# Down projection of a decoder step: second weight parts one slot later, one accumulator in two PSUM tiles by turns, weight loads two pairs ahead, last convolution later

## The chip, the cores and the metric

The program runs on one core of a Trainium2 chip. The metric is the device time of one execution in microseconds (us). Five engines work side by side, each through its own queue in program order: TensorE (PE; its weight loads are shown as PEld), VectorE (DVE), ScalarE (ACT), GpSimd (POOL) and SyncE (SP). SP issues nearly all DMAs of the stage that matters here. Engines wait for one another through semaphores.

## The reference, cut to what matters

One layer of a decoder step for 512 prompt rows and 8 x 8 sample rows, 576 rows in all, held transposed: 128 features on the partitions, 576 rows (two halves of 288) along the free axis. The attention half of the layer is untouched. The stage in question is the end of the channel mixer:

```python
    u = _rms(x, p['g_ffn']) @ p['w_up']
    up = jnp.concatenate([prev.astype(u.dtype), u], axis=1)
    c = p['conv_b'] + p['conv_w'][CONV_W - 1] * up[:, CONV_W - 1:]
    for j in range(CONV_W - 1):
        c = c + p['conv_w'][j] * up[:, j:j + T]
    a, b = jnp.split(c, 2, axis=-1)
    return x + (jax.nn.silu(a) * b) @ p['w_down'], up[:, T:]
```

`w_down` is 5632 x 2048 in float32, and the products have to keep float32's accuracy.

## The kernel before, in words

**Numbers in two parts.** TensorE multiplies in float32r. Each weight tile and each operand is therefore split in a first part (`whi`, a copy on ACT, lines 2217 to 2222, `down_first`) and a second part (`wlo`, source minus first part on DVE, lines 2224 to 2229, `down_second`). A product of a 512 x 128 weight block with a 512 x 288 operand block is three passes of four matmuls: first part with first part, first part with the operand's second part, second part with first part (`down_product`, line 2231). The second part of the weights is read by the third pass alone.

**Up projection, and the joint.** The loop over f = 0..43 in `finish` computes the up projection, convolution and gate. The convolution of f - 1 runs during f; that of f = 43 (`convolve(43, i)`, five steps on ACT, DVE and POOL) follows the loop. Then comes `down`.

**First 512 rows of w_down.** In `down` (line 2496) a loop over `ot` = 0..15 multiplies the first 512 rows directly, 24 matmuls for each `ot`, and adds the result to `hT`. It also prepares the operands of the first chunk (`build(1)`, its steps in the list `todo`).

**The other 5120 rows.** They are five chunks of 1024 rows. Each chunk has eight pairs of output tiles (256 output columns), 40 pairs in all, n = 0..39. A pair is a 2 x 2 x 2 block product done in seven products instead of eight, P1 P6 P5 P7 P2 P3 P4 in this order, 280 slots t in all, with i = t % 7 the place in the pair. Weight blocks: A11, A12 (one 512 KB load into a `raw` buffer of two), A21, A22 (256 KB loads into the shared `z` ring of eight), and four sums on DVE: S1 = A21 + A22, S2 = S1 - A11, S3 = A22 - S2, S4 = A12 - S2 (`down_sum`; S1, S3 and S4 overwrite a block that is no longer needed). P1 takes A11, P6 S2, P5 S1, P7 S3, P2 A12, P3 S4, P4 A22.

**Accumulators.** PSUM holds three of them, `Z[0]` to `Z[2]`: P1 and P2 add in bank 0, P6, P7 and P4 in bank 1, P5 and P3 in bank 2. After every product DVE adds the accumulator as it stands to the rows of `hT` where it belongs (`down_evict`; the result of P1 goes to a tile `Y`, in the first chunk by ACT, later by DVE). The next product of the same bank waits for that. Z[0] and Z[1] are the two tiles `zp`, Z[2] is one of four tiles `fa`.

**One slot t of the loop.** The program order is: first part of the weights of t + 2 (ACT), eviction of product t - 1 (DVE), second part of t + 2 (DVE), a weight sum (DVE, at i = 0, 2, 4, 5), one step of `todo` in seven of eight pairs (i = 3, 6; the operands of the next chunk, on DVE and ACT), at i = 1 the loads for pair n + 1 (SP), then the twelve matmuls of t. In the last chunk each pair also puts out its two tiles (`store_y`: transposes on TensorE into free `fa` tiles, copies, DMA).

The order of each queue is thus written out by the loop; a small clock in the program (`pump`) places only the output's steps.

Of the kernel before, what the change touches and what calls it, by code (L numbers as in the profile page):

```python
# [9 lines left out]
F32 = mybir.dt.float32  # L10
# [10 lines left out]
HB = 288  # L21
# [257 lines left out]
class Kern:  # L279
# [2138 lines left out]
    def finish(self, es, outs, w_down):  # L2418
        nc, a = self.nc, self.a
        self.fpool = self.pool(es, "ffn", side="right")  # L2420
        self.bpool = self.pool(es, "big", side="right")
        self.spawn(self.ffn_consts())
        self.cst, self.ssq, self.W = [None, None], None, {}
        self.B = {name: [[self.operand(name, n, half) for half in range(2)] for n in "hl"]
                  for _, name, _ in self.PRODUCTS.values()}
        order = [o for i in range(8) for o in (i, i + 8)]

        def xload(n):
            if n < 16:
                x = self.z("xr")  # L2430
                nc.sync.dma_start(out=x, in_=self.xT[order[n]])
                return x

        def free(kt):
            if kt == 0:
                self.weights(0, "A11")
                self.weights(0, "A22")
            elif kt in (1, 2):
                self.weights(0, ("A12", "A21")[kt - 1])
            elif kt == 6:  # L2440
                self.U = [self.place(12 + s, (128, FW), "u") for s in range(2)]
                for U in self.U:
                    nc.gpsimd.memset(U[:, 0:2], 0.0)
            elif kt == 7:
                self.C = [self.place(14 + s, (128, FW - 2), "C") for s in range(2)]
                self.first_parts(0, 0)
                self.second_parts()

        def later(kt):
            if kt == 4 and self.rest:  # L2450
                self.rest()
                self.rest = None

        x, self.rest = xload(0), None
        for n, ot in enumerate(order):
            last = n == 15
            ps, = self.gemm([(outs[ot], 128, list(range(8)), self.mixs)],
                            on_kt=lambda kt: (later(kt), last and free(kt)), before=self.mixed)
            nx = xload(n + 1)
            self.out_done(ot, ps, x)  # L2460
            x = nx
        self.rest()
        norm = self.spawn(self.second_norm(), first=True)
        self.Z = [self.zp(), self.zp(), self.ps("fa")]
        self.held.add(self.Z[2].tensor.name)
        self.gs, self.hT = [], {}
        self.gd = self.dram("gd", (128, 44, NT))
        self.st = Stream(self, 2, 4)
        downs = self.add_down(w_down, 0)
        self.w_down = w_down  # L2470
        win = a["win_sample"].rearrange("l b t k g d -> (l b) t (k g d)")
        todo = []
        for f in range(44):
            for i in range(7):
                if f == 0 and i == 3:
                    self.until(lambda: norm.done and not self.threads)
                parts = self.before_slot(f, i)
                if i > 3 and todo:
                    todo.pop(0)()
                self.product(f, i, parts)  # L2480
                if f == 43 and i in (0, 1):
                    todo += self.load_first(i)
            if 2 <= f < 18:
                b, t = (f - 2) // 2, 252 * (f % 2)
                nc.gpsimd.dma_start(out=win[b, t:t + 252],
                                    in_=a["cache_win"][0, b, 8 + t:260 + t].rearrange("t k g d -> t (k g d)"))
        while todo:
            todo.pop(0)()
        self.evict(43, 6)
        for i in range(5):  # L2490
            self.convolve(43, i)
        self.done(self.Z[2])
        self.down(downs)
        self.drain()

    def down(self, downs):
        for ot in range(2):
            self.load_h(ot)
        self.V, self.vs = {}, {}
        Y4 = self.fpool.tile([128, 4, HB], F32, name="Y4", tag="prev")  # L2500
        Y1 = self.fpool.tile([128, HB], F32, name="Y1", tag="cw")
        self.Y = [Y4[:, i] for i in range(4)] + [self.rstd[:, :HB], self.rstd[:, HB:], Y1]
        todo, B = self.build(1)
        for ot in range(16):
            hi, lo = self.st.get(downs[ot])
            o = self.zp()
            for kt in range(4):
                for n, (w, x) in enumerate(((hi, 0), (lo, 0), (hi, 1))):
                    for h in range(2):
                        self.mm(o[:, 512 * h:512 * h + HB], w[:, kt], self.gs[h][x][:, kt],  # L2510
                                kt == 0 and n == 0, kt == 3 and n == 2)
                    if n < 2:
                        self.pump()
            self.st.prep_to(downs[ot] + 5)
            h = self.h2(self.hT[ot])
            self.nc.vector.tensor_tensor(h, self.halves(o), h, ALU.add)
            if ot + 2 < 16:
                self.load_h(ot + 2)
            if 0 < ot < 15:
                todo.pop(0)()  # L2520
            if ot == 11:
                self.down_weights(0, 1)
            elif ot == 13:
                self.down_weights(0, 0)
            elif ot == 14:
                self.down_sum(0, "S1")
                self.down_first(0)
                self.down_sum(0, "S2")
                self.down_second(0)
                self.down_first(1)  # L2530
        self.down_second(1)
        self.Z = [self.zp(), self.zp(), self.ps("fa")]
        self.held.add(self.Z[2].tensor.name)
        for t in range(280):
            n, i = t // 7, t % 7
            if t % 56 == 0 and t:
                B = nextB
            if t % 56 == 0 and t < 224:
                todo, nextB = self.build(2 + t // 56)
            self.down_first(t + 2)  # L2540
            if t:
                self.down_evict(t - 1)
            self.down_second(t + 2)
            for m, name in {0: ((n, "S3"),), 2: ((n, "S4"),), 4: ((n + 1, "S1"),), 5: ((n + 1, "S2"),)}.get(i, ()):
                self.down_sum(m, name)
            if n % 8 and i in (3, 6) and todo:
                todo.pop(0)()
            if i == 1:
                self.down_weights(n + 1, 1)
                self.down_weights(n + 1, 0)  # L2550
            self.down_product(t, B)
        self.down_evict(279)

# [75 lines left out]
```

## Time and profile before

| | us |
|---|---|
| median of 3 runs | 2978.86 (2977.79 to 2979.95) |
| the profiled execution | 2977.68 |
| its span, first to last instruction | 2975.9 |

| engine | busy us | share of the span |
|---|---|---|
| PE | 2880.6 | 97% |
| PEld | 2839.7 | 95% |
| DVE | 2221.1 | 75% |
| ACT | 1459.3 | 49% |
| POOL | 390.3 | 13% |

The mean granted TensorE clock is 0.993. In the page's forty slices PE is at nine tenths or more nearly everywhere, and at eight tenths in most of the last seven, with DVE at eight or nine there. Those slices are the seven-product loop, which begins at 2435.15 us of the span. The shares of the whole span say little about it, so the rows below are taken from that stretch and from the joint before it. In a timeline row the first number is the start, the second the length, both in us, then engine, operation, output and inputs, count, and in brackets the idle time before it with what ended it. Rows of matmuls overlap, because matmuls are pipelined; the distance between starts is what counts.

### The profile page before, as it was taken

How to read it: one execution, taken by the hardware profiler on the slowest of the kernel's cores; microseconds unless marked ns; L12 is line 12 of the kernel's file. 1: busy time of each engine (PE TensorE's matmuls, PEld its weight loads, DVE VectorE, ACT ScalarE, POOL GpSimd, SP SyncE). 2: the span in 40 equal slices, each digit the busy share in tenths (PEclk: the TensorE clock that was granted, in tenths of full speed). 3: DMA queues.
4: the chain of work that ended last, by engine and by line, in shares of the span. 5: the costliest groups of instructions: out<-in, count | busy, mean ns of one | idle time of the engine just before them, and what ended most of it. 6: DMA issues, size and time to landing. Idle time of an engine off the chain costs nothing.

```text
span 2975.9 us, 56967 instructions
## 1 busy us (share of the span) xinstructions
PE 2880.6 (97%) x21370; PEld 2839.7 (95%) x21370; DVE 2221.1 (75%) x4403; ACT 1459.3 (49%) x2863; POOL 390.3 (13%) x681
## 2 busy tenths in 40 slices
PE   8999999999999999999999999999999998888889
PEld 7999999999999999999999999999999998888889
DVE  4332456766476566468999999999999978888888
ACT  6443568666354555334544454454454534333333
POOL 3011131312301111200111111111110100000000
PEclk9999999999999999999999999999999999999999
DMA  8443333222554566755444543433433452342333
GB/s 246 130 113 82 107 102 89 88 83 78 139 157 126 177 207 220 244 174 176 125 133 124 144 134 110 126 99 109 122 101 109 137 188 81 105 117 79 101 92 109
DMA packets 560143, 385.79 MB, mean 130 GB/s; under 512 B 65477, under 2 KB 527893, under 8 KB 559613
## 3 DMA queue, kind: packets, MB, share of 16 engines
q1 hardware_dynamic: 537068, 308.29, 36.5%
q0 software_dynamic: 22768, 73.86, 7.5%
q8 instruction: 169, 2.77, 0.4%
q14 instruction: 106, 0.86, 0.1%
q10 hardware_dynamic: 32, 0.01, 0.0%
HBM read 316.51 MB, written 75.32 MB: 132 GB/s over the span
## 4 chain that ended last, share of the span: by engine, by line
PE 54%; DVE 10%; issue 5%; ACT 3%; POOL 1%; DMA 0%; ACTq 0%; DVEq 0%; POOLq 0%
PE zp L189 39%; PE fa L189 15%; DVE wlo L189 3%; ACT whi L189 2%; DVE hT L189 1%; DVE s L189 1%; DVE t L189 1%; DVE a L189 1%; DVE raw L189 1%; POOL ret_sample L189 0%; DMA raw<-w_down 0%; DVE B22l L189 0%; POOL mix L189 0%; DVE T2l L189 0%; DVE B11l L189 0%
## 5 line engine op out<-in xcount | busy, mean ns | idle before, releaser
L189 ACT ACTIVATE whi<-raw 128x512 fp32r<-128x512 f32 x588 | 356.0, 625 | 460.7 <-PE zp L189 242.4
L189 DVE TENSOR_TENSOR wlo<-raw,whi 128x512 fp32r<-128x512 f32 x584 | 398.2, 697 | 118.7 <-ACT whi L189 116.1
L189 PE MATMUL zp<-ah,whi 128*128 128x288 f32 (+1 forms) x2208 | 480.9, 299 | 2.1 <-ACT whi L189 1.9
L189 PE MATMUL zp<-al,whi 128*128 128x288 f32 (+1 forms) x2208 | 478.1, 298 | 0.1
L189 PE MATMUL zp<-ah,wlo 128*128 128x288 f32 x2176 | 473.8, 299 | 3.1 <-DVE wlo L189 3.1
L189 ACT ACTIVATE whi<-s 128x512 fp32r<-128x512 f32 x256 | 156.3, 631 | 437.0 <-DVE s L189 343.9
L189 PEld LDWEIGHTS zp<-ah,whi 128*128 128x128 f32 (+1 forms) x2208 | 356.3, 189 | 5.5 <-ACT whi L189 2.3
L189 PEld LDWEIGHTS zp<-ah,wlo 128*128 128x128 f32 x2176 | 351.4, 189 | 6.4 <-DVE wlo L189 3.9
L189 PEld LDWEIGHTS zp<-al,whi 128*128 128x128 f32 (+1 forms) x2208 | 354.7, 188 | 1.8 <-DVE al L189 0.3
L189 ACT ACTIVATE whi<-a 128x512 fp32r<-128x512 f32 x344 | 202.2, 625 | 122.5 <-DVE u L189 78.2
L189 DVE TENSOR_TENSOR wlo<-a,whi 128x512 fp32r<-128x512 f32 x344 | 225.2, 687 | 29.0 <-ACT whi L189 26.2
L189 DVE TENSOR_TENSOR wlo<-s,whi 128x512 fp32r<-128x512 f32 x256 | 168.6, 687 | 28.2 <-ACT whi L189 28.2
L189 PE MATMUL zp<-T2h,whi 128*128 128x288 f32 x576 | 105.3, 301 | 51.5 <-DVE hT L189 51.4
L189 DVE SCALAR_TENSOR_TENSOR C<-u,cw,C 128x592 f32<-128x592 f32 x176 | 146.4, 832 | 3.1
L189 PEld LDWEIGHTS zp<-T2h,whi 128*128 128x128 f32 x576 | 84.4, 189 | 57.6 <-issue 30.5
L189 DVE CUSTOM_DVE_ANT_0 P<-fa,th 128x256 f32<-128x256 f32 (+3 forms) x128 | 60.9, 488 | 63.6 <-PE fa L189 61.7
L189 PE MATMUL zp<-T2h,wlo 128*128 128x288 f32 x576 | 103.4, 301 | 0.0
L189 PE MATMUL zp<-B11h,wlo 128*128 128x288 f32 x576 | 100.6, 294 | 2.3 <-DVE wlo L189 2.3
L189 PE MATMUL zp<-B11h,whi 128*128 128x288 f32 x576 | 100.3, 294 | 1.3 <-ACT whi L189 1.3
L189 DVE TENSOR_TENSOR hT<-zp,hT 128x288 f32<-128x288 f32 (+1 forms) x191 | 90.4, 478 | 14.5 <-PE zp L189 11.8
L189 PE MATMUL zp<-T2l,whi 128*128 128x288 f32 x576 | 101.2, 296 | 0.0
L189 PE MATMUL zp<-B11l,whi 128*128 128x288 f32 x576 | 100.2, 294 | 0.0
(435 smaller groups left out, 6640.1 us busy)
## 6 DMA issues: line engine op xcount, KB each, us to landing
a<-w_up SPq DMA_DIRECT2D x264, 256.0 KB
raw<-w_in SPq DMA_DIRECT2D x102, 512.0 KB
raw<-w_down SPq DMA_DIRECT2D x48, 512.0 KB
raw<-w_up SPq DMA_DIRECT2D x44, 512.0 KB
a<-w_down SPq DMA_DIRECT2D x80, 256.0 KB
raw<-w_out SPq DMA_DIRECT2D x32, 512.0 KB
gd<-g POOLq DMA_DIRECT2D x44, 288.0 KB, 2.9
xr<-xT SPq DMA_DIRECT2D x32, 288.0 KB
```

The costliest lines, as they stand in the source:

```text
L189: return fn(*a, **kw)
```

## The change

Five edits, all in `finish` and `down`:

- The second part of a weight tile is made in slot t for t + 1 (`down_second(t + 1)`) and no longer for t + 2. First parts stay at t + 2.
- Bank 1 has two tiles by turns: `Z = [A, bs[n % 2], C]`, set after the eviction of the last product of the pair before. A and `bs[0]` are the `zp` tiles, `bs[1]` and C are `fa` tiles, so two `fa` tiles are left for the output's transposes instead of three.
- The loads of weights are issued for pair n + 2, `raw` at i = 5 and A21, A22 at i = 6, instead of all for n + 1 at i = 1. Pairs 0 and 1 are loaded at `ot` = 11 to 14.
- The convolution of f = 43 runs inside the first two rounds of the `ot` loop, after the preparation of the weights, instead of ahead of the loop. The tiles `Y` are placed after the loop for that reason.
- The sums S1, S2 of pair 0 and its first weight parts come after the `ot` loop instead of at `ot` = 14, and `build` for the next chunk stands after the slot's other work.

```diff
         self.evict(43, 6)
-        for i in range(5):
-            self.convolve(43, i)
         self.done(self.Z[2])
...
             self.st.prep_to(downs[ot] + 5)
+            for i in ((0, 1), (2, 3, 4))[ot] if ot < 2 else ():
+                self.convolve(43, i)
             h = self.h2(self.hT[ot])
...
-            if ot == 11:
-                self.down_weights(0, 1)
-            elif ot == 13:
-                self.down_weights(0, 0)
-            elif ot == 14:
-                self.down_sum(0, "S1")
-                self.down_first(0)
-                self.down_sum(0, "S2")
-                self.down_second(0)
-                self.down_first(1)
-        self.down_second(1)
-        self.Z = [self.zp(), self.zp(), self.ps("fa")]
-        self.held.add(self.Z[2].tensor.name)
+            if ot in (11, 12):
+                self.down_weights(ot - 11, 1)
+            elif ot in (13, 14):
+                self.down_weights(ot - 13, 0)
...
+        self.down_sum(0, "S1")
+        self.down_sum(0, "S2")
+        for t in range(2):
+            self.down_first(t)
+        self.down_second(0)
+        A, C = self.zp(), self.ps("fa")
+        self.held.add(C.tensor.name)
+        bs = self.zp(), self.ps("fa")
+        self.held.add(bs[1].tensor.name)
         for t in range(280):
             n, i = t // 7, t % 7
             if t % 56 == 0 and t:
                 B = nextB
-            if t % 56 == 0 and t < 224:
-                todo, nextB = self.build(2 + t // 56)
             self.down_first(t + 2)
             if t:
                 self.down_evict(t - 1)
-            self.down_second(t + 2)
+            if i == 0:
+                self.Z = [A, bs[n % 2], C]
+            self.down_second(t + 1)
             for m, name in {0: ((n, "S3"),), 2: ((n, "S4"),), 4: ((n + 1, "S1"),), 5: ((n + 1, "S2"),)}.get(i, ()):
                 self.down_sum(m, name)
+            if t % 56 == 0 and t < 224:
+                todo, nextB = self.build(2 + t // 56)
             if n % 8 and i in (3, 6) and todo:
                 todo.pop(0)()
-            if i == 1:
-                self.down_weights(n + 1, 1)
-                self.down_weights(n + 1, 0)
+            if i == 5:
+                self.down_weights(n + 2, 0)
+            elif i == 6:
+                self.down_weights(n + 2, 1)
             self.down_product(t, B)
```

DVE's queue from slot 5 of a pair into slot 2 of the next one, before (`s` is S2, then S4; `a` numbers are A21 and A22, A21 holding S1; `raw` is A11 or A12, later S3; `hT` rows are evictions; `t` and `T3l` are a step of `todo`):

```order
L189 TENSOR_TENSOR s_31266<-a_31187,raw 128x512
L189 TENSOR_TENSOR hT<-fa,hT 128x288
L189 TENSOR_TENSOR wlo<-s_31266,whi 128x512
L189 TENSOR_TENSOR t<-T1l,B11l 128x576
L189 TENSOR_TENSOR T3l<-t,T3h 128x576
L189 TENSOR_TENSOR hT<-zp,hT 128x288
L189 TENSOR_TENSOR wlo<-a_31187,whi 128x512
L189 TENSOR_TENSOR raw<-a_31189,s_31266 128x512
L189 TENSOR_TENSOR wlo<-raw,whi 128x512
L189 TENSOR_TENSOR hT<-zp,hT 128x288
```

The same place in the changed kernel:

```order
L189 TENSOR_TENSOR s_31265<-a_31153,raw 128x512
L189 TENSOR_TENSOR hT<-fa,hT 128x288
L189 TENSOR_TENSOR wlo<-raw,whi 128x512
L189 TENSOR_TENSOR t<-T1l,B11l 128x576
L189 TENSOR_TENSOR T3l<-t,T3h 128x576
L189 TENSOR_TENSOR hT<-fa,hT 128x288
L189 TENSOR_TENSOR wlo<-s_31265,whi 128x512
L189 TENSOR_TENSOR raw<-a_31155,s_31265 128x512
L189 TENSOR_TENSOR wlo<-a_31153,whi 128x512
L189 TENSOR_TENSOR hT<-zp,hT 128x288
L189 TENSOR_TENSOR wlo<-raw,whi 128x512
```

The second part of S2 stood one eviction behind the sum that makes S2; now the second part of A11, the step of `todo` and a further eviction stand between. The second part of S3 stood right behind its sum; now two rows stand between.

TensorE's queue in the first pair that uses the second tile of bank 1 (T2, T1 and T3 are the operands of P6, P5 and P7), as a difference:

```order
 L189 MATMUL zp<-B11h,wlo 128x288 x4
-L189 MATMUL zp<-T2h,whi 128x288 x4
-L189 MATMUL zp<-T2l,whi 128x288 x4
-L189 MATMUL zp<-T2h,wlo 128x288 x4
+L189 MATMUL fa<-T2h,whi 128x288 x4
+L189 MATMUL fa<-T2l,whi 128x288 x4
+L189 MATMUL fa<-T2h,wlo 128x288 x4
 L189 MATMUL fa<-T1h,whi 128x288 x4
```

P6, P7 and P4 of every second pair write another tile; no matmul is added or moved.

ACT's queue at the joint between the up projection and the `ot` loop (`C` rows are the convolution of f = 43, `whi` the first parts for the `ot` loop), as a difference:

```order
 L189 ACTIVATE T2h<-T2l 128x1152
-L189 ACTIVATE whi<-raw 128x512 x2
+L189 ACTIVATE whi<-raw 128x512 x5
 L189 ACTIVATE C<-u,cw 128x592 x2
-L189 ACTIVATE C<-C 128x592
-L189 ACTIVATE whi<-raw 128x512 x4
+L189 ACTIVATE whi<-raw 128x512
+L189 ACTIVATE C<-C 128x592
```

Three first parts have moved ahead of the two `C` rows, the third of which reads the third `raw` tile of the `ot` loop.

## Rows read from the trace of the kernel before

**Rows 1.** Busy time by stretch: the five chunks (us, then each engine, clock, DMA).
```profile
2435.15:2544.70 109.55, 93.78 (x674) 90.94 (x673) 88.45 (x158) 42.67 (x74) 0.00 (x0) 0.98 0.39 111
2544.70:2653.11 108.41, 94.30 (x674) 92.21 (x673) 92.04 (x166) 40.48 (x67) 0.00 (x0) 0.97 0.35 100
2653.11:2760.61 107.50, 94.39 (x675) 92.34 (x674) 91.91 (x166) 40.48 (x67) 0.00 (x0) 0.97 0.35 101
2760.61:2869.46 108.85, 94.57 (x674) 92.32 (x673) 92.31 (x166) 40.60 (x67) 0.00 (x0) 0.97 0.35 101
2869.46:2975.90 106.44, 99.81 (x754) 98.90 (x752) 89.72 (x184) 39.55 (x71) 0.00 (x0) 0.97 0.35 101
```

**Rows 2.** Waits of PE, 2435.15 to 2975.9 (total us, times, longest).
```profile
PE zp L189 <- DVE hT L189: 57.9, 39, 2.6
```

**Rows 3.** Timeline of PE, one pair (n = 4).
```profile
2489.99 0.69 PE L189 MATMUL zp<-B11h,whi 128*128 128x288 f32 x4
...
2491.05 0.69 PE L189 MATMUL zp<-B11h,wlo 128*128 128x288 f32 x4
2492.55 0.77 PE L189 MATMUL zp<-T2h,whi 128*128 128x288 f32 x4 [0.81 <-DVE hT L189]
...
2496.59 0.77 PE L189 MATMUL zp<-T3h,whi 128*128 128x288 f32 x4 [0.63 <-DVE hT L189]
...
2503.01 0.69 PE L189 MATMUL zp<-B11h,whi 128*128 128x288 f32 x4
```

**Rows 4.** Timeline of PE, a pair without a wait (n = 9), its start and end.
```profile
2558.06 0.69 PE L189 MATMUL zp<-B11h,whi 128*128 128x288 f32 x4
...
2569.17 0.69 PE L189 MATMUL zp<-B11h,whi 128*128 128x288 f32 x4
```

**Rows 5.** Timeline of DVE around the pair of rows 3.
```profile
2487.04 0.68 DVE L189 TENSOR_TENSOR wlo<-a,whi 128x512 fp32r<-128x512 f32 x1
2487.64 0.68 DVE L189 TENSOR_TENSOR a<-a,a 128x512 f32<-128x512 f32 x1
2488.24 0.45 DVE L189 TENSOR_TENSOR hT<-zp,hT 128x288 f32<-128x288 f32 x1
2488.61 0.68 DVE L189 TENSOR_TENSOR wlo<-raw,whi 128x512 fp32r<-128x512 f32 x1
...
2491.95 0.45 DVE L189 TENSOR_TENSOR hT<-zp,hT 128x288 f32<-128x288 f32 x1
...
2493.92 0.68 DVE L189 TENSOR_TENSOR raw<-a,s 128x512 f32<-128x512 f32 x1
2495.38 0.69 DVE L189 TENSOR_TENSOR wlo<-raw,whi 128x512 fp32r<-128x512 f32 x1 [0.78 <-ACT whi L189]
```

**Rows 6.** Waits of DVE, 2435.15 to 2870.
```profile
DVE wlo L189 <- ACT whi L189: 62.8, 124, 1.6
```

**Rows 7.** DVE's groups in chunks 2 to 4 (busy us, mean ns): steps of `todo`.
```profile
L189 DVE TENSOR_TENSOR t<-B22l,t 128x576 f32<-128x576 f32 x6 | 4.5, 752 | 0.0
...
L189 DVE TENSOR_TENSOR B11l<-B11l,B11h 128x1152 fp32r<-128x1152 f32 x3 | 4.1, 1352 | 0.0
```

**Rows 8.** Timeline of PE after a long wait.
```profile
2523.29 1.16 PE L189 MATMUL fa<-T1h,whi 128*128 128x288 f32 x4
```

**Rows 9.** Timeline of PE, the last chunk's one wait for an eviction.
```profile
2873.24 0.77 PE L189 MATMUL zp<-T2h,whi 128*128 128x288 f32 x4 [2.02 <-DVE hT L189]
```

**Rows 10.** Timelines of PE, DVE, ACT and SP at the joint.
```profile
2387.09 0.40 PE L189 MATMUL zp<-B11h,wlo 128*128 128x288 f32 x1 [2.34 <-DVE wlo L189]
...
2382.20 3.31 DVE L189 SCALAR_TENSOR_TENSOR C<-u,cw,C 128x592 f32<-128x592 f32 x4
...
2381.07 0.89 ACT L189 ACTIVATE C<-u,cw 128x592 f32<-128x592 f32 x1 [3.34 <-DVE u L189]
...
2391.26 1.15 ACT L189 ACTIVATE whi<-raw 128x512 fp32r<-128x512 f32 x2 [5.59 <-DMA raw<-w_down]
...
2387.10 1.54 SPq L189 DMA_DIRECT2D raw<-w_down  x2
```

More of the change, by code (lines that the diff above doesn't have):

```diff
@@ L2499, in down @@
         self.V, self.vs = {}, {}
-        Y4 = self.fpool.tile([128, 4, HB], F32, name="Y4", tag="prev")
-        Y1 = self.fpool.tile([128, HB], F32, name="Y1", tag="cw")
-        self.Y = [Y4[:, i] for i in range(4)] + [self.rstd[:, :HB], self.rstd[:, HB:], Y1]
         todo, B = self.build(1)
@@ L2520, in down @@
                 todo.pop(0)()
-            if ot == 11:
-                self.down_weights(0, 1)
-            elif ot == 13:
-                self.down_weights(0, 0)
-            elif ot == 14:
-                self.down_sum(0, "S1")
-                self.down_first(0)
-                self.down_sum(0, "S2")
-                self.down_second(0)
-                self.down_first(1)
-        self.down_second(1)
-        self.Z = [self.zp(), self.zp(), self.ps("fa")]
-        self.held.add(self.Z[2].tensor.name)
+            if ot in (11, 12):
+                self.down_weights(ot - 11, 1)
+            elif ot in (13, 14):
+                self.down_weights(ot - 13, 0)
+        Y4 = self.fpool.tile([128, 4, HB], F32, name="Y4", tag="prev")
+        Y1 = self.fpool.tile([128, HB], F32, name="Y1", tag="cw")
+        self.Y = [Y4[:, i] for i in range(4)] + [self.rstd[:, :HB], self.rstd[:, HB:], Y1]
+        self.down_sum(0, "S1")
[7 more added lines that the diff above has]
+        self.held.add(bs[1].tensor.name)
         for t in range(280):
```

## Prediction

> **What bounds the kernel now.** I read the busy times by stretch first, then the waits, then single pairs. All edits lie between the joint at about 2381 us and the end of the span, 2975.9. The seven-product loop begins at 2435.15 [rows 1], so it takes 540.75 us in five chunks of 106.4 to 109.6. In chunks 2 to 4 TensorE is busy 92 to 95% and VectorE 92%, at a granted clock of 0.97: two engines, each nearly full, each with holes.
>
> TensorE's holes have one cause: 57.9 us, 39 times, all on evictions [rows 2]. One pair shows how [rows 3]. P1's last pass starts at 2491.05; one pass takes 0.53 (a third of a product, below), so P6 could start at 2491.58. It starts at 2492.55, 0.97 late, because bank 1 still holds P4 of the pair before. That eviction runs from 2491.95 to 2492.40 [rows 5], and TensorE follows 0.15 later. P7 is 0.79 late in the same way (2496.59, bank 1 again). The pair takes 2503.01 - 2489.99 = 13.02. A pair without a wait takes 2569.17 - 2558.06 = 11.11 [rows 4], so 1.59 a product, 0.53 a pass, and a chunk of eight has a floor of 88.9. After a long wait four matmuls take 1.16 instead of 0.69 [rows 8]: that stretch ran at the lower of the two clock levels (1.2 and 2.4 GHz) after an idle stretch, so a wait costs more than its own length.
>
> Why is VectorE late at those evictions? It waits for almost nothing but first parts from ScalarE: 62.8 us, 124 times in four chunks [rows 6], that is 31 times and 15.7 us a chunk. Each is a round trip: sum on VectorE, first part on ScalarE, second part on VectorE. For S3 the sum ends at 2493.92 + 0.68 = 2494.60 and the second part starts at 2495.38, 0.78 later [rows 5]. The loop is thus paced by VectorE's chain of round trips, and TensorE waits for what stands behind it.
>
> **The change part by part.**
>
> *Second parts one slot later.* No instruction is added. Between S2 and its second part there now stand the second part of A11, steps of `todo`, and an eviction. I price them by start distances [rows 5]: 0.60 for a 512-column row (2487.04 to 2487.64), 0.37 for an eviction (2488.24 to 2488.61). So S2 and S4 have 0.37 + 0.60 + 0.37 = 1.34 against the 0.78 needed, and S3 has 0.60 + 0.37 = 0.97. All round trips fit, and the 15.7 us a chunk go. What is left is VectorE's own work: a pair has 11 rows of 512 columns and seven evictions, 11 x 0.60 + 7 x 0.37 = 9.2. A chunk's `todo` has 16 steps of 0.752 and three of 1.352 [rows 7], less the 0.08 overlap seen in rows 5: 16 x 0.67 + 3 x 1.27 = 14.5. With 0.7 for two extra evictions a chunk is 8 x 9.2 + 14.5 + 0.7 = 88.8; in chunk 1, where ScalarE evicts P1, 88.8 - 7 x 0.37 = 86.2. As a check, VectorE's busy 92.0 less some 31 overlaps of 0.085 is 89.4. TensorE's floor is 88.9: the two are balanced.
>
> The Trainium skill speaks against spacing so tight ("VectorE: DVE Perf Modes", "The DRAIN you can't avoid"): the next VectorE operation starts only once the earlier one has emptied. By full row lengths the work of a chunk would be 8 x (11 x 0.69 + 7 x 0.45) + 16 x 0.752 + 3 x 1.352 + 0.9 = 102.9. The rows of 5 show the next row starting 0.08 before the earlier one ends, so I keep the distances, and give this a small chance below.
>
> *Bank 1 in two tiles.* No matmul is added or moved. P6 writes another tile than P4 did, so it waits for an eviction a pair old: the 28 of 39 waits at P6 (the 2.6 us one too) go. P7 still waits for P6's eviction, with one product between: 1.59 - 0.45 - 0.15, less some 0.2 of queue, leaves a slack of about 0.8.
>
> *What is late next.* The second part for t + 1 is now made during t and read by its third pass: it is needed 1.59 + 1.06 = 2.65 after the end of t - 1, and is ready some 1.4 after it (eviction 0.37 after 0.15, second part 0.68, 0.2 for latency): slack 1.2. VectorE's slot is balanced where it holds a sum, 0.62 short of a product without one, and 0.73 too long where two steps of `todo` come. The backlog rises to 0.76 after the first such slot and to 1.55 in the next pair: 0.1 to 0.6 over the slack, at about four points in a chunk. I take 1.5 us a chunk for it. Bounds: nothing, when the floor of 88.9 holds; and 94 a chunk, VectorE's busy sum of 92 [rows 1] plus 2 of start-up, when no overlap helps.
>
> *Sums of pair 0 behind the `ot` loop.* S1 and S2 stand behind the last eviction now; P1's third pass waits for eviction 0.67, two sums 1.20 and the second part 0.68, less what its first two passes cover: +1.8 us, once.
>
> *Loads two pairs ahead.* A21, A22 are issued 5 slots (7.9 us) and `raw` 7 slots (11.1) before their first use, instead of 4 and 3. One load took 4.16 from issue to use (2387.10 to 2391.26) [rows 10], so either lead suffices. On SP they move past the operand loads of `build` at a chunk's start; buffers come free at the latest in slot 3 of the pair. I take nothing; below nothing is possible by the few waits for loads in the first pair, above by a wait for a ring buffer of at most one slot, 1.6.
>
> *The joint.* Before, TensorE waits 2.34 at 2387.09 because the second parts for `ot` = 1 stand behind four C rows (3.31) and the g rows on VectorE [rows 10]. Now the second parts go first and that wait falls. But ScalarE takes the third `raw` tile's first part ahead of the first two C rows, and this waits for its DMA. The buffer comes free after the second parts, about 4 us earlier than before, so issue about 2383 and landing about 2387.2. Then two C rows on ScalarE (0.9 each, partly beside VectorE's), two on VectorE (1.65), then the eviction of `ot` = 0, which ends near 2390.3 to 2391. `ot` = 2 needs its tile at 2387.5: wait 2.8 to 3.6, and 0.2 to 0.3 more at `ot` = 3 behind the next C rows. Net +1.0; bounds -1.6 (DMA lands early enough, some 0.7 left) and +3 (both waits, with slow matmuls after).
>
> *Last chunk.* Its pairs carry transposes and are bound by TensorE; the one wait of 2.02 [rows 9] goes, with some smaller ones: -3 (2.2 to 3.8). Two tiles for transposes instead of three cost nothing while a copy of about 0.6 lies beside 1.6 of products; if each of 16 were exposed, +10.
>
> *Sum.* Chunks 1 to 4: 4 x (88.9 + 1.5) + 1.8 = 363.4, before 109.55 + 108.41 + 107.50 + 108.85 = 434.3: -70.9. Last chunk -3, joint +1: -72.9. The profiled execution took 2977.68 (span 2975.9 and 1.78 around it), so 2904.8; the median of the runs shown is 1.2 above it: **2906**. By its own bounds 2895 (no backlog, -3.8, -1.6) to 2923 (chunks of 94, +3 at the joint).
>
> **The rivals.**
>
> *Half of the round trips stay.* If ScalarE's first part answers later than 0.78 when it stands behind `todo`'s copies, VectorE keeps about half of its 62.8 us of waits and paces the loop. For: it is at 92% in rows 1. Against: ScalarE is busy at most 43%. Half is 31.4, and the 6 of backlog counted above are part of it: +25, so 2931.
>
> *P7's wait takes the place of P6's.* The backlog grows past 0.8 and P7 is late in every pair of chunks 1 to 4: 32 x (0.63 + 0.23 for slow matmuls after) = +27: 2933. For: P7 waits already [rows 3], and its tile still has one product between. Against: S3's round trip, which made it late, is spread.
>
> *No gain.* The Trainium skill ("TensorE: Matmul & The Clock Gate", "HAM oscillation") tells of a kernel in which a double buffer in PSUM gave nothing further. Here that is the case where VectorE's chain itself takes 108 a chunk: 2979. The 15.7 us that VectorE waits in each chunk [rows 6] speak against it.
>
> *VectorE without overlap.* 102.9 a chunk (99.7 in the first): 3 x 102.9 + 99.7 = 408.4, 45 above 363.4: 2952.
>
> *Slower.* The second part, with one product less of lead, misses the third pass in nearly every product: by half of a second part's 0.60: 280 x 0.3 = +84, so 2990. This decides once the second part comes more than 1.2 after the 1.4 worked out, as when VectorE carries a steady backlog over 1.2; balanced sums (88.8 against 88.9) make that possible, and slots without a sum, which give back 0.62, speak against.
>
> **How the numbers follow.** Forecast 0.67, half of the round trips 0.13, P7 0.10, no gain 0.03, no overlap 0.02, slower 0.05. The range 2894 to 2934 takes in the forecast's bounds and the first two rivals; left out are 0.10 for the others and some 0.08 of the forecast's tails. A measurement of this kernel can tell 0.2%, about 6 us, from no change. Faster by more: 0.67 + 0.13 + 0.10 + 0.02 = 0.92; within: 0.03; slower: 0.05.
>
> **What would show it.** Right: waits at P6 gone, few and short ones at P7; VectorE's waits for first parts near nothing and waits for TensorE in their place; pairs of 11.1 to 11.6 us; clock 1.00 in the chunks; at the joint one wait of about 3 us behind C rows, none for second parts; `raw` issued near 2383. Wrong: chunks over 94, waits of the third passes for second parts in most pairs, or waits for loads in the loop.

## The result, and the profile after

The changed kernel takes 2905.98 us (median of 4 runs, 2904.84 to 2912.03) against 2979.4 for the kernel before (4 runs, 2977.79 to 2983.67): a ratio of 0.9756, with a 95% interval of 0.9738 to 0.9773. The prediction was 2906, in a range of 2894 to 2934. That the two medians agree to 0.02 us is luck; the terms are compared one by one below.

The execution that was profiled took 2912.03, with a span of 2910.3: it is the longest of the four. The first matmul of `ot` = 0 starts at 2386.53 in it and at 2381.13 before, after the same instructions, so 5.4 us of its time arose ahead of everything that was changed. Over all profiled executions of this study that start lies between 2376.96 and 2386.53. I therefore compare from that matmul on: 2975.9 - 2381.13 = 594.77 before, 2910.3 - 2386.53 = 523.77 after, -71.0.

The five chunks of the loop, busy time by stretch (columns as in [rows 1]):

```profile
2442.59:2534.05 91.46, 89.71 (x674) 89.00 (x673) 87.38 (x159) 42.59 (x74) 0.00 (x0) 1.00 0.41 117
2534.05:2624.90 90.85, 89.96 (x675) 89.03 (x673) 89.27 (x166) 40.51 (x67) 0.00 (x0) 1.00 0.42 119
2624.90:2715.76 90.86, 89.95 (x675) 89.01 (x673) 89.28 (x166) 40.52 (x67) 0.00 (x0) 1.00 0.43 120
2715.76:2806.63 90.87, 89.95 (x675) 89.01 (x673) 89.28 (x166) 40.51 (x67) 0.00 (x0) 1.00 0.43 120
2806.63:2910.30 103.67, 98.50 (x754) 97.21 (x752) 88.96 (x184) 39.45 (x71) 0.00 (x0) 0.99 0.39 109
```

Beside [rows 1], 17 to 18 us have gone from each of chunks 1 to 4. The counts of instructions are the same; VectorE's busy time fell from 92.0 to 89.3 in the same 166 rows, because rows that follow one another without a wait overlap; the clock rose from 0.97 to 1.00. Both engines are now nearly full at once.

TensorE's waits, 2442 us to the end (total, times, longest), where [rows 2] had 57.9 us in 39 waits for evictions:

```profile
PE zp L189 <- DVE wlo L189: 3.1, 5, 1.7
PE fa L189 <- DVE wlo L189: 1.3, 3, 0.5
PE fa L189 <- DVE hT L189: 0.5, 1, 0.5
```

No wait for an eviction is left in chunks 1 to 4 (the one 0.5 is at the output's end); what is late now, eight times, is a second part. VectorE's waits in chunks 1 to 4, where [rows 6] had 62.8 us in 124 waits for ScalarE:

```profile
DVE hT L189 <- PE zp L189: 5.0, 9, 1.2
DVE hT L189 <- PE fa L189: 2.8, 5, 0.9
DVE wlo L189 <- ACT whi L189: 1.5, 4, 0.5
```

VectorE now waits for TensorE more than for ScalarE. Its timeline at the place where the round trips stood (pairs 9 and 10; `s` is S2, `raw` A11, then S3):

```profile
2554.30 0.68 DVE L189 TENSOR_TENSOR wlo<-a,whi 128x512 fp32r<-128x512 f32 x1
2554.89 0.68 DVE L189 TENSOR_TENSOR s<-a,raw 128x512 f32<-128x512 f32 x1
2555.50 0.45 DVE L189 TENSOR_TENSOR hT<-fa,hT 128x288 f32<-128x288 f32 x1
2555.86 0.68 DVE L189 TENSOR_TENSOR wlo<-raw,whi 128x512 fp32r<-128x512 f32 x1
2556.46 0.75 DVE L189 TENSOR_TENSOR t<-T1l,B11l 128x576 f32<-128x576 f32 x1
2557.13 0.75 DVE L189 TENSOR_TENSOR T3l<-t,T3h 128x576 fp32r<-128x576 f32 x1
2557.80 0.45 DVE L189 TENSOR_TENSOR hT<-fa,hT 128x288 f32<-128x288 f32 x1
2558.17 0.68 DVE L189 TENSOR_TENSOR wlo<-s,whi 128x512 fp32r<-128x512 f32 x1
2558.77 0.68 DVE L189 TENSOR_TENSOR raw<-a,s 128x512 f32<-128x512 f32 x1
2559.37 0.45 DVE L189 TENSOR_TENSOR Y<-zp,Y 128x288 f32<-128x288 f32 x1
2559.74 0.68 DVE L189 TENSOR_TENSOR wlo<-a,whi 128x512 fp32r<-128x512 f32 x1
2560.34 0.45 DVE L189 TENSOR_TENSOR hT<-zp,hT 128x288 f32<-128x288 f32 x1
2560.70 0.68 DVE L189 TENSOR_TENSOR wlo<-raw,whi 128x512 fp32r<-128x512 f32 x1
```

None of the thirteen rows carries a bracket, so VectorE does not wait. S3 is ready at 2558.77 + 0.68 = 2559.45 and its second part starts at 2560.70: 1.25 later, with useful rows between, where [rows 5] had 0.78 of waiting.

TensorE at the joint, at the start of the loop and at the end of a chunk (first matmul of `ot` = 0, `ot` = 2, a matmul behind it, P1's third pass of pair 0, then pair 15 and pair 16):

```profile
2386.53 0.29 PE L189 MATMUL zp<-B11h,whi 128*128 128x288 f32 x1
...
2396.13 0.38 PE L189 MATMUL zp<-B11h,whi 128*128 128x288 f32 x1 [3.07 <-ACT C L189]
...
2397.87 0.44 PE L189 MATMUL zp<-B11h,whi 128*128 128x288 f32 x1
...
2445.53 0.80 PE L189 MATMUL zp<-B11h,wlo 128*128 128x288 f32 x4 [1.72 <-DVE wlo L189]
...
2613.08 0.69 PE L189 MATMUL zp<-B11h,whi 128*128 128x288 f32 x4
...
2617.91 0.80 PE L189 MATMUL fa<-T1h,wlo 128*128 128x288 f32 x4 [0.44 <-DVE wlo L189]
...
2624.90 0.69 PE L189 MATMUL zp<-B11h,whi 128*128 128x288 f32 x4
2628.06 0.80 PE L189 MATMUL zp<-T2h,wlo 128*128 128x288 f32 x4 [0.35 <-DVE wlo L189]
```

Pair 15, the eighth of its chunk, takes 2624.90 - 2613.08 = 11.82; the first of the next chunk takes 11.72. The shortest pairs take 11.10. The wait at `ot` = 2 is behind the C rows, which come late because ScalarE stands at a DMA (SP's issue, then ScalarE):

```profile
2388.31 1.58 SPq L189 DMA_DIRECT2D raw<-w_down  x2
```
```profile
2392.18 0.63 ACT L189 ACTIVATE whi<-raw 128x512 fp32r<-128x512 f32 x1 [5.88 <-DMA raw<-w_down]
2392.72 1.64 ACT L189 ACTIVATE C<-u,cw 128x592 f32<-128x592 f32 x2
```
```profile
2393.61 1.71 DVE L189 SCALAR_TENSOR_TENSOR C<-u,cw,C 128x592 f32<-128x592 f32 x2 [4.13 <-ACT C L189]
2395.24 0.75 DVE L189 TENSOR_TENSOR hT<-zp,hT 128x576 f32<-128x576 f32 x1
```

TensorE's bracket names ScalarE's C rows, but those end at 2394.36. The instruction that ends last ahead of 2396.13 is VectorE's eviction of `ot` = 0, at 2395.24 + 0.75 = 2395.99, behind its own C rows.

### The profile page after: what moved, and what is told of

Read it like the earlier page. It is cut to its first block, busy times and chain, and to the rows that moved or that the text cites. A ratio compares the mean times of both kernels' runs of the same rounds, so it can differ in the third digit from the quotient of the medians.

```text
span 2910.3 us, 56777 instructions
## 1 busy us (share of the span) xinstructions
PE 2866.7 (99%) x21370; PEld 2830.7 (97%) x21370; DVE 2210.2 (76%) x4403; ACT 1459.1 (50%) x2863; POOL 392.3 (13%) x681
## 3 DMA queue, kind: packets, MB, share of 16 engines
q8 instruction: 169, 2.77, 0.4%
## 4 chain that ended last, share of the span: by engine, by line
PE 59%; DVE 7%; issue 4%; POOL 1%; ACT 1%; DMA 0%; POOLq 0%; ACTq 0%; DVEq 0%
PE zp L189 41%; PE fa L189 18%; DVE wlo L189 2%; DVE hT L189 1%; DVE s L189 1%; DVE t L189 1%; POOL ret_sample L189 0%; DVE a L189 0%; DVE raw L189 0%; POOL mix L189 0%; DVE B22l L189 0%; DVE B11l L189 0%; DMA al<-mix 0%; DVE T2l L189 0%; ACT B11h L189 0%
## 5 line engine op out<-in xcount | busy, mean ns | idle before, releaser
L189 POOL COPY u<-prev 128x16 f32<-128x16 f32 x88 | 30.9, 351 | 456.1 <-DVE C L189 428.3
L189 PE MATMUL zp<-T2h,wlo 128*128 128x288 f32 x496 | 87.9, 297 | 1.4 <-DVE wlo L189 1.4
L189 PEld LDWEIGHTS zp<-B11h,whi 128*128 128x128 f32 x576 | 84.7, 188 | 3.3 <-ACT C L189 3.3
L189 PE MATMUL zp<-T2h,whi 128*128 128x288 f32 x496 | 86.8, 295 | 0.0
L189 PEld LDWEIGHTS zp<-B11h,wlo 128*128 128x128 f32 x576 | 84.8, 188 | 2.0 <-DVE wlo L189 2.0
```

The lines of the kernel that those rows point to most:

```text
L189: return fn(*a, **kw)
```

## The experiments

Theory A, that of the prediction: VectorE's round trips through ScalarE set the pace, and making second parts one slot later takes them away. Theory B: bank 1 in one tile was the bound, and the second tile brought the gain. The table is worked out from the traces: the joint runs from the first matmul of `ot` = 0 to the loop, the loop to the end of the span, the third column is chunk 2 (chunk 3 for e7_extra_behind, where a record is missing). Medians are of 4 to 10 runs. Brackets behind a time hold its ratio to the kernel before, with the 95% interval.

| kernel | joint | loop | chunk 2 | median |
|---|---|---|---|---|
| before | 54.02 | 540.75 | 108.4 | 2979.4 |
| changed | 56.06 | 467.71 | 90.85 | 2905.98 |
| b1_tiles_alone | 55.18 | 538.80 | 107.8 | 2975.73 |
| e1_one_tile | 55.74 | 472.24 | 91.92 | 2910.98 |
| e2_second_ahead | 55.73 | 536.12 | 108.7 | 2972.4 |
| e4_loads_one_ahead | 55.54 | 468.48 | 90.86 | 2906.51 |
| e5_conv_before | 55.33 | 467.76 | 90.88 | 2904.61 |
| e3_joint_split | 51.70 | 467.66 | 90.88 | 2901.0 |
| e7_extra_behind | 55.73 | 467.72 | 90.85 | 2905.49 |
| e8_todo_single | 55.82 | 464.52 | 89.94 | 2903.48 |
| e9_all_four | 51.90 | 462.77 | 89.97 | 2897.09 |
| e11_no_triples | 51.88 | 461.81 | 90.04 | 2896.82 |
| e12_less_todo | 51.70 | 459.0 | 89.12 | 2894.08 |
| e10_todo_pool | 51.84 | 475.04 | 92.95 | 2908.4 |

**b1_tiles_alone**, the kernel before with the second tile alone:

```diff
-        self.Z = [self.zp(), self.zp(), self.ps("fa")]
-        self.held.add(self.Z[2].tensor.name)
+        A, C = self.zp(), self.ps("fa")
+        self.held.add(C.tensor.name)
+        bs = self.zp(), self.ps("fa")
+        self.held.add(bs[1].tensor.name)
...
+            if i == 0:
+                self.Z = [A, bs[n % 2], C]
```

> The kernel before with bank 1 in two tiles by turns and nothing else changed. Theory A: VectorE's queue still needs its busy 92 and 15.7 of waits a chunk; the waits of TensorE at P6 go but come back at P7, at other evictions or at second parts: 2960 to 2979, at most 18 us better. Theory B: the 28 waits at P6 go with their slow matmuls: 2935 to 2945.

The ratio to the kernel before is 0.9989, interval 0.998 to 0.9999. TensorE's waits in the loop:

```profile
PE zp L189 <- DVE hT L189: 24.0, 17, 1.7
PE fa L189 <- ACT whi L189: 18.7, 18, 1.6
PE fa L189 <- DVE hT L189: 18.0, 13, 1.5
```

The sum is 61 us, where [rows 2] had 57.9; the waits stand at other instructions (P7 and P5 in the place of P6). Taking away the wait that the trace named brought 0.1%. This is theory A.

**e2_second_ahead**, the changed kernel with the second tile, but second parts for t + 2:

```diff
         self.down_second(0)
+        self.down_second(1)
...
-            self.down_second(t + 1)
+            self.down_second(t + 2)
```

> The changed kernel with second parts made for t + 2 again (one slot earlier), the two tiles of bank 1 kept. Theory A: VectorE waits for ScalarE's first parts again, about 31 times and 15.7 us a chunk; its own work of 88.8 a chunk leaves no room for them, so chunks 1 to 4 take 100 to 106 and the time is 2945 to 2965. Theory B: the two tiles keep TensorE free of waits, 2906 to 2915.

2972.4, ratio 0.9981 (0.9971 to 0.999): nearly all of the gain is gone, theory A. I had left too much room, though; the loop is slower than A's 2945 to 2965. VectorE's waits, and one of TensorE's:

```profile
DVE wlo L189 <- ACT whi L189: 65.1, 129, 1.6
```
```profile
2575.03 0.78 PE L189 MATMUL zp<-T3h,whi 128*128 128x288 f32 x4 [1.41 <-DVE hT L189]
```

One of the 129 waits, 0.5, is in the last chunk already; a quarter of the other 64.6 is 16.2. With it VectorE's 88.8 becomes 105, and each of some 31 rows behind a wait also loses its overlap of 0.08 with the row before: 2.5 more, 107.5, against 107.4 to 108.7 in the chunks of its trace. The T3h row is P7, which now waits for P6's eviction: the rival of the prediction in which P7's wait takes P6's place does happen, where the round trips stay.

**e1_one_tile**, the changed kernel with one tile for bank 1:

```diff
-                self.Z = [A, bs[n % 2], C]
+                self.Z = [A, bs[0], C]
```

> The changed kernel with bank 1 back in one tile (P6, P7 and P4 of every pair write the same one); all else as changed. Theory A (VectorE's chain of round trips made the evictions late, and the later second parts cured it): P4's eviction is now first in its slot and ends about 0.6 us after P4, while P6 starts 1.59 after it; waits at P6 only where the extra evictions of an eighth pair have left a backlog. 2906 to 2912 us, chunks 1 to 4 at 91 to 92.5. Theory B (the single tile of bank 1 was the bound): the 28 waits at P6 come back, about 1 to 1.5 us each with slow matmuls behind them: 2935 to 2950, chunks at 98 to 101.

2910.98 (0.9774, 0.9758 to 0.979), inside A's range; chunk 1 takes 92.67, a little above it. TensorE's waits in chunks 1 to 4:

```profile
PE zp L189 <- DVE hT L189: 7.0, 11, 0.9
```

They stand at P6 in the fourth, the sixth and the first pair of a chunk, not only behind the eighth as I had expected: by the estimate made before the run P4's eviction leaves P6 some 0.8 us of slack, and the double steps of `todo`, two of which stand in the third and two in the fifth pair, probably use it up as well. So the second tile is worth about 4.5 us of the loop (472.24 - 467.71) once second parts come late, and about 2 without that (540.75 - 538.80), in one execution each.

**e4_loads_one_ahead**, all loads for n + 1 at i = 1:

```diff
-            if i == 5:
-                self.down_weights(n + 2, 0)
-            elif i == 6:
-                self.down_weights(n + 2, 1)
+            if i == 1:
+                self.down_weights(n + 1, 1)
+                self.down_weights(n + 1, 0)
```

> The changed kernel with the weight loads one pair ahead again (all at slot 1 for the next pair). Theory A: a load takes about 4 us and the first sum comes 4.8 us after issue, the first part of A11 6.4 after it: 2905 to 2909, no waits for loads but perhaps in the first pair. Rival: buffers of the ring come free later than slot 1 or loads land late beside the operand loads, and VectorE waits 0.5 to 1 us in most pairs, which its full queue passes on to TensorE: 2920 to 2940.

2906.51, chunks 2 to 4 within 0.02 of the changed kernel's. One load is waited for, in the first pair (1.8 us on VectorE), and chunk 1 takes 92.30 instead of 91.46. The longer lead is worth nothing beyond these 0.8 us.

**e5_conv_before**, the five convolution steps ahead of the `ot` loop again:

```diff
         self.evict(43, 6)
+        for i in range(5):
+            self.convolve(43, i)
...
-            for i in ((0, 1), (2, 3, 4))[ot] if ot < 2 else ():
-                self.convolve(43, i)
```

> The changed kernel with the convolution of f = 43 ahead of the ot loop again, as before the change. If the joint cost what its trace shows: the wait of 3.07 us and its slow matmuls turn back into the one of 2.34, the stretch from the first matmul of ot = 0 to the loop falls from 56.06 to about 54, time 2903 to 2905. If the later place of Y or the sums costs too, it stays at 55 or more: 2905 to 2907.

2904.61 is in the first guess, a joint of 55.33 in the second. The wait is that of [rows 10] to 0.01 us, but this time slow matmuls follow it:

```profile
2390.07 0.40 PE L189 MATMUL zp<-B11h,wlo 128*128 128x288 f32 x1 [2.35 <-DVE wlo L189]
...
2391.36 0.44 PE L189 MATMUL zp<-T2l,whi 128*128 128x288 f32 x1
```

In e5 the sums of pair 0 and the place of Y also differ from before, but b1, whose code at the joint is that of before, shows the same: 55.18, with slow matmuls behind the wait.

```profile
2388.28 0.40 PE L189 MATMUL zp<-B11h,wlo 128*128 128x288 f32 x1 [2.36 <-DVE wlo L189]
...
2389.05 0.45 PE L189 MATMUL zp<-B11h,whi 128*128 128x288 f32 x1
```

So the same idle time costs 1.2 to 1.3 us more in two executions than in another. Against these two, the six executions with the new joint (55.54 to 56.06) take 0.2 to 0.9 more, not the 2.0 that the two first traces show.

**e3_joint_split**, the third `raw` tile's first part behind the C rows:

```diff
-            self.st.prep_to(downs[ot] + 5)
+            self.st.prep_to(downs[ot] + (5 if ot else 4))
             for i in ((0, 1), (2, 3, 4))[ot] if ot < 2 else ():
                 self.convolve(43, i)
+            self.st.prep_to(downs[ot] + 5)
```

> The changed kernel with the third raw tile's first part behind the first two convolution rows of f = 43 on ScalarE, not ahead of them. If the wait at the joint comes from that first part's wait for its DMA: ScalarE's C rows start 5 us earlier, the 3.07 us wait of TensorE at ot = 2 goes with the slow matmuls behind it (about 1.0), the stretch from the first matmul of ot = 0 to the loop falls from 56.06 to 52 to 53, time 2901 to 2903. If the C rows themselves (3.3 us on VectorE) are what delays the eviction, a wait of 1 to 3 us stays at ot = 2 or 3: 2904 to 2907.

2901.0 (0.9736, 0.9721 to 0.9751), joint 51.70; TensorE waits 0.4 us in it. That is 0.3 better than the best guess for the joint. So the wait came from ScalarE's stand at the DMA, and the C rows themselves fit beside two rounds of `ot`.

**e7_extra_behind**, the two extra evictions of P1 in the eighth pair moved behind the second part of the slot:

```diff
-                for x in (a[1], b[1], b[0]):
-                    add(x, bank)
+                add(a[1], bank)
+                self.extra = lambda: (add(b[1], bank), add(b[0], bank))
...
             self.down_second(t + 1)
+            if n % 8 == 7 and i == 1:
+                self.extra()
```

> The changed kernel with the two extra evictions of P1 in every eighth pair behind the second part of the same slot, not ahead of it. If these two (0.74 us) make the two longest pairs of a chunk (the eighth at 11.8, the next first at 11.7, against 11.10): both fall to 11.1 to 11.3, the waits of third passes for second parts go, about 1.2 us a chunk: 2901 to 2904. If the double steps of todo make the backlog, the pairs stay at 11.5 or more: 2905 to 2907.

A miss: 2905.49, the loop 467.72 against 467.71. The time is that of the second guess, but the double steps are not its reason, as e8 shows. The second part of P5 is in time now, and P7 waits instead, for P6's eviction, which stands behind the moved ones:

```profile
2612.09 0.77 PE L189 MATMUL fa<-T3h,whi 128*128 128x288 f32 x4 [0.38 <-DVE hT L189]
```

**e8_todo_single**, one VectorE row in a step of `todo`, and slot 1 as a third place for them:

```diff
-            yield lambda: (temp("T1", c, b12, b11), second("T3", c, t["T3"]))
+            yield lambda: temp("T1", c, b12, b11)
+            yield lambda: second("T3", c, t["T3"])
...
-            if n % 8 and i in (3, 6) and todo:
+            if n % 8 and i in ((1, 3, 6) if n % 8 < 7 else (3, 6)) and todo:
```

(the other two double steps are cut in the same way, and the steps ahead of the loop are taken two at a time where needed).

> The changed kernel with the steps of todo that held two VectorE rows cut in two, and a third place for them in a pair (slot 1) in pairs 1 to 6 of a chunk. If the double steps make the backlog, as the prediction had it: pairs 3, 5 and 6 of a chunk fall from 11.5 and 11.25 to 11.1 and the eighth from 11.8 to 11.3, 1 to 1.5 us a chunk: 2900 to 2903. If the extra evictions make most of it: pairs 3, 5, 6 fall by 0.7 in all and the eighth and first stay: 2903 to 2905.

2903.48, loop 464.52. In chunks 2 to 4 all pairs but two fall to 11.10 or 11.11; the eighth goes from 11.8 to 11.59, the first stays at 11.7. That is the second guess: the double steps cost 0.8 us a chunk (467.71 - 464.52 = 3.2 over four), and the end of the chunk another 1.1.

**e9_all_four**: e3, e7 and e8 together, and S1, S2 of pair 0 with their parts at `ot` = 14.

> The changed kernel with four edits: first part of the third raw tile behind the C rows, extra evictions behind the second part, steps of todo one VectorE row each, and S1, S2 of pair 0 with their parts at ot = 14. If VectorE's place of work is all that is left above TensorE's floor: joint -4, first pair -1.7, chunks 1 to 4 at 88.9 to 89.3 instead of 90.9, -7: 2892 to 2896. If the balance of 88.8 against 88.9 leaves a backlog wherever the work stands, chunks stay at 90 or more: 2898 to 2902.

2897.09 (0.9722, 0.9709 to 0.9735): between the two guesses. Joint and first pair (13.09 to 11.38) came as expected; chunk 1 takes 89.27, and chunks 2 to 4 stopped at 90.0.

**e11_no_triples**: as e9, with the three 1152-column rows of `todo` cut in halves and spread.

```diff
-        todo += [lambda: (second("B11", al, x["B11"]), first("B22", al, x["B22"])),
-                 lambda: second("B21", al, x["B21"]), lambda: second("B22", al, x["B22"])]
+        todo = s1 + [both(lo("B11", c1), lo("B22", c1)), lo("B21", c1)] + s2[:6] + [
+            both(s2[6], lo("B11", c2)), s2[7], lo("B22", c2), lo("B21", c2)]
```

> As e9_all_four, with the three 1152-column second parts of todo cut in halves of 576 and spread, so that the eighth pair has single rows of 576 only; VectorE's sum stays the same (3 x 0.07 us more). If the place of these rows makes the late pairs: the eighth and the next first pair fall from 11.6 and 11.7 to 11.1 to 11.3, 2893 to 2896. If it is VectorE's sum over the chunk: they stay within 0.2 of 11.6 and 11.7, 2896 to 2898.

2896.82 (0.9723, 0.971 to 0.9736). The first pair falls to 11.1, and the fifth and seventh rise to 11.34 and 11.37, the eighth to 11.73: the lateness moved, as neither guess had it, and the chunk stayed at 90.04. Chunk 1, where ScalarE evicts P1 and VectorE is busy for 86.7, takes 88.99, TensorE's floor. So the place of these rows among the later pairs makes no difference to the chunk's time. That VectorE's sum over the whole chunk is the bound does not follow, however: the sum is 89.05 in 90.04. The first pair of chunk 2, and its last four:

```profile
2518.98:2530.09 11.11, 11.11 (x87) 11.11 (x86) 10.31 (x20) 4.63 (x9) 0.00 (x0) 1.00 1.05 317
2563.42:2609.02 45.60, 45.22 (x339) 44.58 (x337) 45.60 (x87) 19.86 (x35) 0.00 (x0) 1.00 0.33 90
```
```profile
DVE hT L189 <- PE zp L189: 1.0, 2, 0.5
```

In the last four pairs VectorE has no hole, and they take 1.2 more than four of 11.11. Its only two waits in the chunk, 1.0 us together, are in the first pair and at its end, and `n % 8` in the code keeps new steps of `todo` out of the first pair. A chunk with some of them there is a rival that no run tried; whether their operands, whose loads are issued in that pair, would be there in time is not known. This is the shortest complete version of the study, level with e9.

**e12_less_todo**: as e11, with four VectorE rows fewer a chunk (second parts of B21 and B22 left out in chunks 2 to 5, so that this part of the products is missing).

```diff
-        lo = lambda n, c: lambda: second(n, c, x[n][:, c])
+        lo = lambda n, s: lambda: second(n, s, x[n][:, s]) if c == 1 or n == "B11" else None
```

> As e11_no_triples, but the second parts of B21 and B22 are left out in chunks 2 to 5 (four VectorE rows of 576 in each of chunks 1 to 4, 2.7 us of VectorE's time a chunk; this part of the products is then not computed). No other engine loses a row. If VectorE's sum per chunk is what holds chunks 2 to 4 at 90.0 instead of TensorE's floor of 88.9: 88.9 to 89.0 in each, 3 us less in all, 2892 to 2895. If it is the place of the extra evictions in the eighth pair, or ScalarE's round trips: the eighth pair stays at 11.7 and the chunks at 89.5 or more.

2894.08. Chunk 2 of e11 and of e12:

```profile
2518.98:2609.02 90.04, 89.66 (x675) 89.02 (x673) 89.05 (x169) 40.77 (x71) 0.00 (x0) 1.00 0.43 120
```
```profile
2522.26:2611.38 89.12, 89.09 (x674) 88.89 (x673) 86.73 (x164) 40.78 (x71) 0.00 (x0) 1.00 0.43 122
```

VectorE has 2.3 us less to do and the chunk is 0.92 shorter, 0.2 above the floor; the eighth pair, still 11.37, keeps that rest. So VectorE's work held the chunk. The rows that are gone stood in the fifth pair (two), in the eighth, and at the start of the next first pair, so this run does not tell VectorE's sum over the chunk from its share in the late pairs.

**e10_todo_pool**: as e9, with 8 of the 16 subtractions of `todo` a chunk on GpSimd.

```diff
+        eng = self.nc.gpsimd if c > 1 else self.nc.vector
+        minus = lambda out, a, b: eng.tensor_tensor(out, a, b, ALU.subtract)
...
-            self.sub(t[n], p, q)
+            minus(t[n], p, q)
```

> As e9_all_four, with 8 of the 16 subtractions of todo in each chunk on GpSimd, which is idle in the loop (5.4 us a chunk off VectorE; GpSimd took 1.6 to 1.9 us for such a row elsewhere in the trace of before). If VectorE's sum is what is left above TensorE's floor: all pairs at 11.10 to 11.2, chunks 1 to 4 at 88.9 to 89.2 instead of 90.0, 2892 to 2895. If only the place of the two 1152-column rows in the eighth pair counts: the eighth and first pair stay at 11.6 and 11.7, 2896 to 2898. If GpSimd's rows slow VectorE's or hold ScalarE's first parts back: over 2899.

2908.4, 11 us slower than e9: the third guess. GpSimd's rows and VectorE's in the fourth pair of chunk 2:

```profile
2556.52 1.45 POOL L189 TENSOR_TENSOR t<-B21l,t 128x576 f32<-128x576 f32 x1 [11.86 <-ACT whi L189]
2557.93 1.90 POOL L189 TENSOR_TENSOR t<-B22l,T1l 128x576 f32<-128x576 f32 x1
```
```profile
2556.68 1.84 DVE L189 TENSOR_TENSOR wlo<-s,whi 128x512 fp32r<-128x512 f32 x1
2558.44 1.94 DVE L189 TENSOR_TENSOR raw<-a,s 128x512 f32<-128x512 f32 x1
```

The second part (0.68 elsewhere) begins 0.16 after GpSimd's first row and ends 0.55 after it; the sum likewise ends 0.55 after the second one (2560.38 against 2559.83). VectorE lost 2.4 us there and saved 2 x 0.67. Over chunk 2 its busy time is 92.02 in 158 rows (e9: 89.03), where 8 rows of 0.67 fewer would have made 83.7:

```profile
2521.32:2614.27 92.95, 90.75 (x675) 89.08 (x673) 92.02 (x158) 39.62 (x67) 13.49 (x8) 1.00 0.42 117
```

VectorE waits for ScalarE's first parts only 1.1 us in chunks 1 to 4, so the stretched rows are the reason and not late first parts. The Trainium skill ("SBUF — State Buffer", "SBUF: two separate sides") states that a VectorE operation with two inputs in SBUF and a GpSimd operation that reads SBUF lock each other out of a port pair for a whole instruction; both stretched rows have two such inputs, and their ends agree with that.

## Why the prediction was right

Point by point, measured in the profiled pair:

- *Chunks 1 to 4*: 363.4 predicted, 91.46 + 90.85 + 90.86 + 90.87 = 364.04 measured. That the round trips go and VectorE's own 88.8 remain held: its busy time is 89.3, or 89.05 in e11. e2 and b1 show that this step carries nearly all of the gain. The opening of the prediction read [rows 1] wrongly, though: 92 to 95 for TensorE, 92 for VectorE and, among the rivals, 43 for ScalarE are us of a chunk, not percent. Of chunks of 107.5 to 108.9 TensorE's 94.3 to 94.6 are 87 to 88%, VectorE's 92 are 85%, and ScalarE has at most 39%. The sums are in us throughout, so the forecast does not change. Beside its 39 waits for evictions TensorE also had one of 1.3 us for a first part and one of 0.4 at the end of the output.
- *Late second parts*: 1.5 us a chunk predicted, 90.86 - 88.9 = 2.0 measured in chunks 2 to 4, and 0.6 in chunk 1 beside pair 0. The size was about right, the place only in part: the double steps cost 0.8 a chunk (e8); the rest I had not placed. It arises at a chunk's end, where the extra evictions and 1152-column rows fall together on a VectorE without reserve in these pairs. e7 and e11 show that moving either by a little moves the lateness, e12 that less work removes most of it. The idle 1.0 us in the first pair (e11) is left as an untested remedy.
- *Pair 0*: 1.8 predicted, 13.09 - 11.11 = 1.98 measured. The terms as written, 0.67 + 1.20 + 0.68 less 1.06 for two passes, give only 1.5; the steps from engine to engine, which have no term, make up most of the rest.
- *Last chunk*: -3 predicted, 103.67 - 106.44 = -2.77 measured. Two transposing tiles cost nothing that shows.
- *Joint*: +1.0 predicted, +2.04 in the profiled pair, 0.2 to 0.9 against e5 and b1. Mechanism and place were as predicted: the `raw` issue 1.8 us after the first matmul of `ot` = 0, a wait of 3.07 (2.8 to 3.6 predicted); the small second wait at `ot` = 3 did not come. What the pair adds is slow matmuls, which the kernel before happened not to have after its own wait.
- *Loads*: nothing predicted, nothing found beyond the 0.8 us of chunk 1 (e4).

The sum was -72.9, and -71.0 was measured in the profiled pair; the medians differ by 73.4. So the mechanism was right and the terms came within about 1 us each, while the exact hit of the median is luck: the single execution from which the sum starts lies 1 to 2 us below the medians, and its joint was 1.2 to 1.3 us shorter than in the two others with the same wait. The lower bound of 2895 is also counted from the 2904.8 of that execution, the upper one from 2906.

The rivals: VectorE keeps 1.5 us of waits for ScalarE in chunks 1 to 4, not half of 62.8. P7 does not wait in them, though it does in e2 and e7, so its slack is thin. A chunk of VectorE rows without overlap would have taken 102.9 and takes 90.9. The same section of the Trainium skill ("VectorE: DVE Perf Modes", "The DRAIN you can't avoid") also states, which the prediction left out, that a next operation that is not held back until the earlier ones have finished starts earlier. The rows agree with that: each starts some 0.08 before the end of the one ahead. That the second tile alone brings no gain did come true, in b1; that VectorE's chain would stay as long did not.

## What to carry to other kernels

A wait names the instruction that came last, not the one that sets the pace: here TensorE waited for evictions, a second accumulator tile removed just that wait, and 0.1% came of it. Look at what the engine waited for is itself waiting for; a round trip to another engine inside an in-order queue is removed by putting other work between its two ends. Once two engines are balanced to 1%, moving work from one full place to another only moves the wait; look first for a stretch where the engine still has a hole. Before handing work to a third engine, see whether its rows stretch those of the engine that is to be relieved.

## What the runs showed of the hardware

VectorE rows of 512 columns take 0.68 us and follow one another every 0.60 where nothing is waited for. Beside GpSimd's two-input rows (1.45 and 1.90 us), VectorE's rows with two inputs in SBUF took 1.84 and 1.94 instead of 0.68. After a wait of 2.34 to 2.36 us at the same place of the joint, matmuls ran at their usual 0.29 in one execution (before) and at 0.44 to 0.45 in two others (e5, b1), with a difference of 1.2 to 1.3 us in the stretch.
